# Sixteen more tokens served by gathered rows in a two-layer trunk, and chunks split two ahead

## The chip, the cores and the metric

The kernel runs on one core of one Trainium2 chip. The time is the device time of one execution in microseconds (us), from runs on the chip. The engines are PE (TensorE, matmuls; PEld is its weight load), DVE (VectorE), ACT (ScalarE), POOL (GpSimd) and SP (SyncE, which issues loads); a name with q behind it (ACTq, SPq) is an engine's issue of DMAs.

## What is computed

The reference is a two-layer trunk on 512 tokens of width 1024. Each layer adds a mixer (attention, a short convolution, gated linear attention) and then a PEER block, which takes most of the time:

```python
def peer(xn, w_q, keys1, keys2, u, v):
    q = (xt @ w_q).reshape(T, PEER_HEADS, 2, PEER_HALF)
    ...
    v1, i1 = lax.top_k(s1, PEER_TOPK)
    v2, i2 = lax.top_k(s2, PEER_TOPK)
    cand = (v1[..., :, None] + v2[..., None, :]).reshape(...)
    sc, ci = lax.top_k(cand, PEER_TOPK)
    ...
    experts = (e1 * PEER_NKEYS + e2).reshape(T, hk)
    gates = jax.nn.softmax(sc, axis=-1).reshape(T, hk)
    ...
        ub = jnp.take(u, eb, axis=0)
        hb = jax.nn.gelu(jnp.einsum('tkd,td->tk', ub, xb), approximate=False)
        vb = jnp.take(v, eb, axis=0)
        return jnp.einsum('tk,tkd->td', gb * hb, vb)
```

Every token picks 128 of 16384 experts (8 heads of 16). An expert has one row of u and one of v, 1024 wide. The inner value of an expert is gelu of the token's dot product with its u row; the output is the sum of the v rows, weighted with gate times inner value.

## The kernel before, in words

**Two ways through PEER.** For tokens 0 to 383 (three blocks of 128, TD = 384) the kernel is dense: it works out the inner values of all 16384 experts, in 128 chunks of 128 experts, and multiplies them with a gate matrix that is zero where an expert was not picked. For tokens 384 to 511 (block 3) it gathers the picked rows: `gathered` (L739) fetches 128 u rows, one for each of a token's picks, by an indirect DMA on POOL's queue (L735), takes the dot product with the normed token (`xg`) on DVE (L743), and then fetches 128 v rows and adds them up in `yacc` on DVE (L752). Four row buffers are in flight (NROW).

**Matmuls in three parts.** `mm3` (L73) makes one float32 product of three: high times high (L75), low or high parts crossed (L76, L77). The high part is ACT's copy of the raw tile, the low part DVE's subtraction (`split`, L649 to L651). So a chunk of hidden values (`hidden`, L659) is 8 x 3 = 24 matmuls, with the u chunk as weights and 384 tokens as columns, into one of two PSUM tiles of pool psB (`psh`), which ACT's Gelu then moves to a tile `ht` (L665).

**First loop** (L785 on, c from 0 to NPRE + LAG - 1 = 74). In each turn: load u chunk c+3 on SP's queue, split chunk c+1, `hidden(c)`, and for c under 72 store the result to DRAM (H, L789, on ACT's queue). Around that, DVE works through a generator `routing`: top-16 and routing of a token block (`route`), then for 16 tokens at a time a `gate_matrix`: four one-hot multiplies on DVE (L984 to L987), 32 matmuls into `psg` (L993, L994), four ACT copies to `stg` (L996) and a store into G in DRAM (L997, 512-byte pieces, 1 MB). Each yield of the generator says what it costs DVE, and a turn goes on until the sum passes `DVE_STEP * (c + 1)`. A step's matmuls and its store come out when the generator is resumed. Once block 3 is routed, `tick(RATE[0])` sends RATE[0] gathered rows a turn.

**Second loop** (L858 on, 128 turns). Turn i adds chunk order[i] to six PSUM tiles `pv`: 3 x 2 x 3 = 18 matmuls of 512 columns, weights `wh`, `wl` (gate times inner value, L833, L835) and columns `vh`, `vl` (the v chunk, L821, L826). The first 56 chunks in the order are 72 to 127, whose hidden values are computed three turns ahead in this loop; the others come back from H. G is read eight chunks at a time (`load_g`, L811), which has to wait for all stores into G. A turn also sends gathered rows: 2.8 in the first 56 turns, then 0.88. What is left is run after the loop, then block 3 gets `yacc` (L879), its sum of squares is taken on ACT (L173) and rsqrt on DVE (L161 to L168); the last two chunks are added block by block. The next layer's norm takes block 3 first (ORDER, L185, transposes L189 into `psn`); at the end of the kernel the scale into `fy` (L1006) and the store do.

**What sets the order.** Most instructions stand in program order on their engine: `pin` holds an instruction to the order in which it was written, `free` leaves it to the scheduler, and rows of a tick are put behind the last low part. Each engine runs its own list in order, so a wait holds all that is behind it. The buffers: three u highs and lows (NUW), three raw u (NUR), six `ht` (NHT), two `wh` and `wl` (NW).

## Time and profile before

| | us |
|---|---|
| median of 3 runs | 3046.72 (3039.78 to 3049.19) |
| the profiled execution | 3044.03 |
| its span, first to last instruction | 3042.3 |
| PE busy in it | 2971.3 |
| DVE busy in it | 2443.7 |
| ACT busy in it | 1268.9 |
| POOL busy in it | 736.2 |

The profile is of one execution: its span is the time from the first to the last instruction, 1.7 us less than the time of that execution, and 4.4 us less than the median of the runs. Matmuls are pipelined, so the busy time of one is longer than the distance to the next start; the distance tells the pace. A busy share is a mean over stages with different limits.

### The profile page before, as it was taken

The numbers are of one execution on the slowest core, as the hardware profiler recorded it, in microseconds if no ns is written. First come the engines' busy times: TensorE is split into PE (matmuls) and PEld (weight loads), VectorE is DVE, ScalarE is ACT, GpSimd is POOL, SyncE is SP. The second block draws the span as 40 slices with busy tenths as digits, with TensorE's granted clock in tenths as the row PEclk, the third lists the DMA queues.
The fourth block names the chain that finished last, engine by engine and source line by source line (L and its number), as shares of the span: only waits on it lengthen the run. The fifth ranks groups of instructions, "written<-read, shape, count | busy, mean of one in ns | idle before, by whom it ended". The sixth has DMA issues, their size and how long they took to land.

```text
span 3042.3 us, 45583 instructions
## 1 busy us (share of the span) xinstructions
PE 2971.3 (98%) x16742; PEld 2659.7 (87%) x16742; DVE 2443.7 (80%) x5057; ACT 1268.9 (42%) x1874; POOL 736.2 (24%) x553
## 2 busy tenths in 40 slices
PE   7999999999999999999999999999999999999998
PEld 7977889999999998788889788999999999988886
DVE  5766999987788787877766769999868788878777
ACT  5343346556333333333353533555553333323333
POOL 0000000222455544322100000002225555542221
PEclk9999999999999999999999999999999999999999
DMA  4212247799989888999722212578999899889996
GB/s 122 67 58 70 98 143 255 271 307 335 348 321 333 322 324 309 362 335 330 282 78 67 73 65 96 169 242 295 314 351 335 323 321 338 330 295 353 333 348 232
DMA packets 335696, 756.64 MB, mean 249 GB/s; under 512 B 31568, under 2 KB 192240, under 8 KB 331376
## 3 DMA queue, kind: packets, MB, share of 16 engines
q1 hardware_dynamic: 141936, 406.60, 37.2%
q0 software_dynamic: 73728, 268.47, 24.7%
q10 hardware_dynamic: 119808, 78.66, 8.2%
q8 instruction: 131, 2.15, 0.3%
q14 instruction: 93, 0.76, 0.1%
HBM read 672.89 MB, written 80.74 MB: 248 GB/s over the span
## 4 chain that ended last, share of the span: by engine, by line
PE 79%; DVE 6%; issue 4%; ACT 4%; DMA 3%; POOL 2%; ACTq 1%; SPq 0%; POOLq 0%; DVEq 0%
PE pv L77 10%; PE pv L76 10%; PE pv L75 10%; PE psh L75 9%; PE psh L77 9%; PE psh L76 9%; PE psp L77 2%; PE psp L76 2%; PE psp L75 2%; PE psq L76 2%; PE psq L77 2%; PE psq L75 2%; POOL row L735 2%; DMA row<-in_v_rows,idx 1%; ACTq L789 1%
## 5 line engine op out<-in xcount | busy, mean ns | idle before, releaser
L735 POOL DMA_INDIRECT row<-in_u_rows,idx x256 | 389.1, 1520 | 1326.3 <-DVE si L893 679.3
L75 PE MATMUL psh<-ahi,uh 128*128 128x384 f32 x2048 | 694.5, 339 | 10.1 <-ACT ht L665 10.1
L77 PE MATMUL psh<-ahi,ul 128*128 128x384 f32 x2048 | 689.2, 337 | 6.6 <-DVE ul L651 6.6
L76 PE MATMUL psh<-alo,uh 128*128 128x384 f32 x2048 | 688.4, 336 | 0.0
L75 PE MATMUL pv<-vh,wh 128*128 128x512 f32 x1536 | 597.7, 390 | 10.4 <-ACT wh L835 10.4
L77 PE MATMUL pv<-vh,wl 128*128 128x512 f32 x1536 | 600.4, 391 | 0.0
L76 PE MATMUL pv<-vl,wh 128*128 128x512 f32 x1536 | 599.9, 391 | 0.0
L735 POOL DMA_INDIRECT row<-in_v_rows,idx x256 | 329.1, 1286 | 604.1 <-DVE yacc L752 568.3
L650 ACT CAST uh<-uraw 128x1024 fp32r<-128x1024 f32 x288 | 302.7, 1053 | 319.8 <-PE psh L76 154.4
L651 DVE TENSOR_TENSOR ul<-uraw,uh 128x1024 fp32r<-128x1024 f32 x288 | 350.4, 1220 | 98.9 <-ACT uh L650 85.5
L75 PEld LDWEIGHTS psh<-ahi,uh 128*128 128x128 f32 x2048 | 387.1, 189 | 16.2 <-ACT ht L665 11.9
L77 PEld LDWEIGHTS psh<-ahi,ul 128*128 128x128 f32 x2048 | 386.6, 189 | 7.2 <-DVE ul L651 7.2
L76 PEld LDWEIGHTS psh<-alo,uh 128*128 128x128 f32 x2048 | 387.0, 189 | 4.1
L821 DVE TENSOR_TENSOR vl<-vraw,vh 128x1024 fp32r<-128x1024 f32 x256 | 312.5, 1221 | 86.5 <-issue 66.5
L665 ACT ACTIVATE ht<-psh 128x384 f32<-128x384 f32 x256 | 125.3, 489 | 613.6 <-PE psh L77 601.1
L75 PEld LDWEIGHTS pv<-vh,wh 128*128 128x128 f32 x1536 | 288.9, 188 | 69.3 <-ACT wh L835 12.0
L77 PEld LDWEIGHTS pv<-vh,wl 128*128 128x128 f32 x1536 | 288.9, 188 | 61.6 <-DVE wl L821 1.1
L76 PEld LDWEIGHTS pv<-vl,wh 128*128 128x128 f32 x1536 | 289.0, 188 | 58.6 <-DVE vl L821 0.5
L752 DVE SCALAR_TENSOR_TENSOR yacc<-row,wk,yacc 128x1024 f32<-128x1024 f32 x254 | 325.7, 1282 | 11.0 <-DMA row<-in_v_rows,idx 9.5
L743 DVE SCALAR_TENSOR_TENSOR gscr<-row,xg 128x1024 f32<-128x1024 f32 x256 | 312.5, 1221 | 13.0 <-DMA row<-in_u_rows,idx 11.3
L835 ACT CAST wh<-ht 128x384 fp32r<-128x384 f32 x256 | 130.7, 510 | 383.2 <-PE pv L76 236.3
L826 ACT CAST vh<-vraw 128x1024 fp32r<-128x1024 f32 x256 | 268.7, 1050 | 26.6 <-DMA vraw<-in_v_rows 24.5
(289 smaller groups left out, 4406.8 us busy)
## 6 DMA issues: line engine op xcount, KB each, us to landing
uraw<-in_peer_u SPq DMA_DIRECT2D x256, 512.0 KB
vraw<-in_v_rows SPq DMA_DIRECT2D x256, 512.0 KB
G<-stg ACTq DMA_DIRECT2D x48, 1024.0 KB
g<-G SPq DMA_DIRECT2D x32, 1536.0 KB
H<-ht ACTq DMA_DIRECT2D x144, 192.0 KB
ht<-H SPq DMA_DIRECT2D x144, 192.0 KB
wraw<-in_w_in SPq DMA_DIRECT2D x96, 256.0 KB
uraw<-in_peer_w_q SPq DMA_DIRECT2D x32, 512.0 KB
```

Of the source, the lines that this page charges most:

```text
L75: mm(ps, ah, bh, start=first, stop=False)
L76: mm(ps, ah, bl, start=False, stop=False)
L77: mm(ps, al, bh, start=False, stop=last)
L650: pin(nc.scalar.copy(hi, src))
L651: self.last = pin(nc.vector.tensor_tensor(lo, src, hi.bitcast(F32), op=OP.subtract))
L665: pin(nc.scalar.activation(hs[c], ps, AF.Gelu))
L735: nc.gpsimd.indirect_dma_start(out=r, out_offset=None, in_=ins[name], in_offset=bass.IndirectOffsetOnAxis(ap=idx[:, k:k + 1], axis=0))
L743: nc.vector.scalar_tensor_tensor(sc, r, 1.0, xg, op0=OP.mult, op1=OP.mult, accum_out=hd[:, k:k + 1])
L752: nc.vector.scalar_tensor_tensor(yacc, r, wk[:, k:k + 1], yacc, op0=OP.mult, op1=OP.add)
L821: self.last = pin(nc.vector.tensor_tensor(lo, src, hi.bitcast(F32), op=OP.subtract))
L826: pin(nc.scalar.copy(vh[c], vs[c]))
L835: pin(nc.scalar.copy(wh[c], hs[c]))
```

## The change

The first 16 tokens of block 0 (NX) leave the hidden matmuls, which go from 384 to 368 columns. Their 128 u rows a token are gathered instead, in 16 steps of 128 rows: `regroup` spreads 16 tokens by 128 picks over 128 partitions by small DMAs on POOL's queue, `xx` holds the normed tokens eight times over, and `extra` makes dot, Gelu and gate and brings the products back. The products then enter the gate matrix of these tokens in place of the gates, as three bfloat16 parts, and in the second loop the 16 columns of `ht` are copied from `g` by ACT instead of multiplied. Apart from that, u is loaded four and split two chunks ahead (one more buffer), `w_hi` is made two turns ahead (one more `wh`), G is read one turn sooner, the first loop takes 80 + 3 chunks instead of 72 + 3, and the rates are others.

```diff
-NPRE = 72
+NPRE = 80
-NHT = 6
+NHT = 5
-NUW = 3
+NUW = 4
-RATE = (0.8, 2.8, 0.88)
-DVE_STEP = 2.72
+RATE = (0.7, 2.8, 0.95)
+DVE_STEP = 2.62
+NX = 16
...
+            xx = pp.tile([P, D], F32, tag="yacc", name="xx")
...
             def hidden(c, pin=pin):
                 uh, ul = uw.pop(c)
-                ps = self.psB.tile([P, TD], F32, tag="b", name="psh")
+                ps = self.psB.tile([P, TD - NX], F32, tag="b", name="psh")
                 for k in range(KD):
-                    self.mm3(ps, uh[:, k], ul[:, k], xh[:, k, 0:TD], xl[:, k, 0:TD], k == 0, k == KD - 1)
+                    self.mm3(ps, uh[:, k], ul[:, k], xh[:, k, NX:TD], xl[:, k, NX:TD], k == 0, k == KD - 1)
                 hs[c] = spare.pop() if spare else new_h()
-                pin(nc.scalar.activation(hs[c], ps, AF.Gelu))
+                pin(nc.scalar.activation(hs[c][:, NX:], ps, AF.Gelu))
...
+                    nc.vector.scalar_tensor_tensor(xx[0:NX], self.x[0:NX, 0], self.rs[0][0:NX], xg[0:NX],
+                                                   op0=OP.mult, op1=OP.mult)
+                    n = NX
+                    while n < P:
+                        nc.gpsimd.dma_start(xx[n:2 * n], xx[0:n])
+                        n *= 2
...
+            def dot(k, xg=xg, hd=hd, idx=idx):
+                r = rows("u_rows", k, idx)
+                sc = gp.tile([P, D], F32, tag="gscr", name="gscr", bufs=1)
+                nc.vector.scalar_tensor_tensor(sc, r, 1.0, xg, op0=OP.mult, op1=OP.mult, accum_out=hd[:, k:k + 1])
...
+            def ahead(c):
+                load_u(c + 4)
+                split_u(c + 2, free)
+                hidden(c, free)
+                if c < NPRE:
+                    nc.scalar.dma_start(H[c], hs.pop(c)[:, NX:])
+
+            ahead(0)
+            best(NQ - 1)
...
+                def extra(gt):
...
+                    regroup(lambda p, s: nc.gpsimd.dma_start(ix[p], idx0[0:NX, s]))
+                    regroup(lambda p, s: nc.gpsimd.dma_start(gx[p], gt[0:NX, s]))
+                    yield 0.1
+                    for k in range(w):
+                        dot(k, xx, hx, ix)
+                        yield 1.25
+                    nc.scalar.activation(hx, hx, AF.Gelu)
+                    nc.vector.tensor_tensor(hx, hx, gx, op=OP.mult)
+                    regroup(lambda p, s: nc.gpsimd.dma_start(wx[0:NX, s], hx[p]))
+                    yield 0.3
...
                         for bt in range(P // TBAT):
-                            yield from self.gate_matrix(tb * (P // TBAT) + bt, E1, E2, GH, GL, G, hp)
+                            if tb == 0 and bt < NX // TBAT:
+                                continue
+                            yield from self.gate_matrix(tb * (P // TBAT) + bt, E1, E2, (GH, GL), G, hp)
+                            for _ in range(3):
+                                yield next(more, 0)
+                        if tb == 1:
+                            for w in more:
+                                yield w
+                            for bt in range(NX // TBAT):
+                                yield from self.gate_matrix(bt, E1, E2, [w3[:, i] for i in range(3)], G, hp, BF16, 1.0)
...
                 for c in range(NPRE + LAG):
-                    load_u(c + 3)
-                    split_u(c + 1, free)
-                    hidden(c, free)
-                    if c == 0:
-                        best(NQ - 1)
-                    if c < NPRE:
-                        nc.scalar.dma_start(H[c], hs.pop(c))
+                    if c:
+                        ahead(c)
...
-                pin(nc.vector.tensor_tensor(htv, htv, gt[c // GE][:, :, c % GE * TBAT:c % GE * TBAT + TBAT], op=OP.mult))
-                wh[c] = vp.tile([P, TD], F32R, tag="wh", name="wh", bufs=NW)
+                pin(nc.scalar.copy(htv[:, 0:b], gv[:, 0:b]))
+                pin(nc.vector.tensor_tensor(htv[:, b:], htv[:, b:], gv[:, b:], op=OP.mult))
+                wh[c] = vp.tile([P, TD], F32R, tag="wh", name="wh", bufs=NW + 1)
                 pin(nc.scalar.copy(wh[c], hs[c]))
...
-            for i in range(3):
-                at(load_v, i)
+            for i in range(4):
+                if i < 3:
+                    at(load_v, i)
                 at(load_g, i)
+            at(w_hi, 0)
             at(v_hi, 0)
+            at(w_hi, 1)
             at(v_hi, 1)
             at(v_lo, 0)
-            at(w_hi, 0)
             at(w_lo, 0)
             for i, c in enumerate(order):
                 rate = RATE[1] if c >= NPRE else RATE[2]
-                load_u(NPRE + i + LAG + 3)
+                load_u(NPRE + i + LAG + 4)
                 at(load_v, i + 3)
-                at(load_g, i + 3)
-                split_u(NPRE + i + LAG + 1)
+                at(load_g, i + 4)
+                split_u(NPRE + i + LAG + 2)
                 if i + LAG < NF:
                     hidden(order[i + LAG])
                 tick(rate / 2)
-                at(w_hi, i + 1)
-                at(v_hi, i + 2)
                 at(v_lo, i + 1)
                 at(w_lo, i + 1)
+                at(w_hi, i + 2)
+                at(v_hi, i + 2)
```

`gate_matrix` takes a list of parts, multiplies the one-hot tile by each and adds as many matmuls for a token; its yield is now 1.15 for each of its DVE steps (4.6 for two parts, as before). The pool of the query stage is closed before the routing pools open, and `yacc` takes the buffer of `xx`.

## Rows read from the trace of the kernel before

**Rows 1.** The page: span; busy us (share) xinstructions of each engine.
```profile
span 3042.3 us, 45583 instructions
...
PE 2971.3 (98%) x16742; PEld 2659.7 (87%) x16742; DVE 2443.7 (80%) x5057; ACT 1268.9 (42%) x1874; POOL 736.2 (24%) x553
```

**Rows 2.** Timeline of PE: start and duration (us), engine, line, operation, operands, shape.
```profile
159.35 0.28 PE L77 MATMUL psp<-wh,alo 128*128 128x256 f32 x1
...
160.42 0.28 PE L77 MATMUL psp<-wh,alo 128*128 128x256 f32 x1
...
599.32 0.33 PE L75 MATMUL psh<-ahi,uh 128*128 128x384 f32 x1
...
602.27 0.34 PE L77 MATMUL psh<-ahi,ul 128*128 128x384 f32 x1
...
1299.43 0.39 PE L75 MATMUL pv<-vh,wh 128*128 128x512 f32 x1
...
1302.83 0.39 PE L75 MATMUL pv<-vh,wh 128*128 128x512 f32 x1
```

**Rows 3.** Waits of PE: waiter <- releaser: us in total, times, longest.
```profile
PE pv L75 <- ACT wh L835: 10.4, 4, 4.6
PE psh L75 <- ACT ht L665: 10.1, 5, 3.3
PE psh L77 <- DVE ul L651: 6.6, 2, 3.3
```

**Rows 4.** Windows, instructions on psh: stretch, length, busy us (count), clock, DMA share, GB/s.
```profile
392.70:434.30 41.60, 36.07 (x192) 34.67 (x192) 3.40 (x7) 0.96 0.35 131
740.40:773.70 33.30, 30.92 (x168) 30.48 (x168) 3.28 (x7) 0.95 0.96 353
2249.30:2280.10 30.80, 29.58 (x168) 29.05 (x168) 2.93 (x6) 1.00 1.02 377
```

**Rows 5.** Groups by line: instructions xcount | busy us, mean ns | idle before, releaser.
```profile
L75 PE MATMUL psh<-ahi,uh 128*128 128x384 f32 x2048 | 694.5, 339 | 10.1 <-ACT ht L665 10.1
...
L752 DVE SCALAR_TENSOR_TENSOR yacc<-row,wk,yacc 128x1024 f32<-128x1024 f32 x254 | 325.7, 1282 | 11.0 <-DMA row<-in_v_rows,idx 9.5
...
L826 ACT CAST vh<-vraw 128x1024 fp32r<-128x1024 f32 x256 | 268.7, 1050 | 26.6 <-DMA vraw<-in_v_rows 24.5
```

**Rows 6.** Windows, all instructions: busy us (count) of PE, PEld, DVE, ACT, POOL.
```profile
392.70:434.30 41.60, 36.99 (x204) 35.85 (x203) 40.28 (x161) 17.05 (x24) 0.00 (x0) 0.96 0.35 131
```

**Rows 7.** Tiles psg, G, g near the first hand-over: count, ns min/median/max, first to last start.
```profile
L994 PE MATMUL psg<-ohl,ohb x80: 218/218/218, 701.8 to 740.4; 128*128 128x128 f16 x80
...
L997 ACTq DMA_DIRECT2D G<-stg x24: 377/377/423, 443.7 to 744.5; - x24
L811 SPq DMA_DIRECT2D g<-G x2: 330/356/383, 758.6 to 808.1; - x2
...
L833 DVE TENSOR_TENSOR ht<-ht,g x7: 552/553/554, 772.4 to 812.3; 128x384 f32<-128x384 f32 x7
```

**Rows 8.** The chain that ended last: start, us on the chain, what (two DMAs).
```profile
2252.72 12.94 DMA G<-stg
...
1211.04 7.68 DMA row<-in_v_rows,idx
```

**Rows 9.** Timeline around the end of both layers: start, us, engine, line, instruction.
```profile
1506.43 1.28 DVE L752 SCALAR_TENSOR_TENSOR yacc<-row,wk,yacc 128x1024 f32<-128x1024 f32 x1
...
1514.38 0.55 DVE L821 TENSOR_TENSOR wl<-ht,wh 128x384 fp32r<-128x384 f32 x1
...
1521.24 0.39 PE L77 MATMUL pv<-vh,wl 128*128 128x512 f32 x1
1521.47 1.03 PE L189 MATMUL psn<-ident,kT 128*128 128x128 f32 x8
...
3030.08 0.39 PE L77 MATMUL pv<-vh,wl 128*128 128x512 f32 x1
...
3037.23 1.28 DVE L1006 SCALAR_TENSOR_TENSOR fy<-x,ry,fg 128x1024 f32<-128x1024 f32 x1
```

More of the change, by code (lines that the diff above doesn't have):

```diff
@@ L95, in setup @@
         self.rstd = {}
[L96 removed]
+        self.rs = {tb: cp.tile([P, 1], F32, name=f"rs{tb}") for tb in (0, TB - 1)}
         self.ident = cp.tile([P, P], F32, name="ident")
@@ L181, in norm_T @@
             rstd = self.rstd.pop(tb) if tb in self.rstd else self.x_rstd(tb, sq)
-            if keep is not None and tb == TB - 1:
-                nc.vector.tensor_copy(keep, rstd)
+            if keep is not None and tb in keep:
+                nc.vector.tensor_copy(keep[tb], rstd)
             xn = xns[j % len(xns)]
@@ L729, in peer, with rows @@
             wk = pp.tile([P, P], F32, name="wk")
-            yacc = pp.tile([P, D], F32, name="yacc")
-            gp = pc.enter_context(tc.tile_pool(name="gather", bufs=1, reuse_waits="tile"))
-            def rows(name, k):
+            def rows(name, k, idx=idx):
                 r = gp.tile([P, D], F32, tag="row", name="row", bufs=NROW)
@@ L753, in gathered @@
                     yield
+            yacc = None
             side = gathered()
@@ L768, in routing @@
                 def routing():
+                    more = None
                     for tb in range(TB):
@@ new lines, in gate_matrix @@
+        t0 = bt * TBAT
+        ng = OHT // 2
+        tok = lambda t: bc(t[:, t0:t0 + OHT], [[2, ng], [0, P], [1, 2]])
+        io = bc(self.iota2, [[0, ng], [2, P], [1, 2]])
+        B = hp.tile([P, ng, P, 2], dt, tag="ohb", name="ohb")
+        A = hp.tile([P, ng, P, 2], F16, tag="oha", name="oha", bufs=1)
+        nc.vector.tensor_tensor(A, io, tok(E1), op=OP.is_equal)
+        nc.vector.tensor_tensor(B, io, tok(E2), op=OP.is_equal)
+        AW = []
+        for i, part in enumerate(parts):
+            AW.append(hp.tile([P, ng, P, 2], dt, tag=("ohh", "ohl")[i % 2], name="ohw"))
+            nc.vector.tensor_tensor(AW[i], A, tok(part), op=OP.mult)
@@ new lines, in gate_matrix @@
+        yield 1.15 * (2 + len(parts))
+        for g in range(OHT // 4):
+            ps = self.psA.tile([P, 4, P], F32, tag="a", name="psg")
+            for j in range(4):
+                at = (slice(None), g * 2 + j // 2, slice(None), j % 2)
+                for i, a in enumerate(AW):
+                    nc.tensor.matmul(ps[:, j], B[at], a[at], start=i == 0, stop=i == len(AW) - 1)
+            nc.scalar.activation(stg[:, :, g * 4:g * 4 + 4].rearrange("p e t -> p t e"), ps, AF.Copy, scale=scale)
```

84 lines of the change are left out of this document (46 added, 38 removed).

## The prediction

> **What bounds the kernel now.** I read the page first: TensorE is busy for 98% of the span [rows 1]. A busy PE is not yet a PE at its peak, so I then took the distance between the starts of neighbouring matmuls from the timeline of PE [rows 2]. The reader is to see three constant cadences: ten matmuls of 256 columns start in nine steps from 159.35 to 160.42 us (0.119 us each), eighteen of 384 columns in seventeen steps from 599.32 to 602.27 us (0.1735 us), sixteen of 512 columns in fifteen steps from 1299.43 to 1302.83 us (0.2267 us). Each column costs 0.42 ns in both intervals. So the time follows what PE streams, wherever PE is fed. Where it isn't, the view of waits names the causes: evictions by ACT (ht), lows by DVE (ul), and wh [rows 3]. These sums are small, but a window shows more than a sum of waits. From 392.7 to 434.3 us PE did 192 matmuls into psh, eight chunks, which at 0.1735 us are 33.3 us of the 41.6; the granted clock there was 0.96, so part of the loss is a stretch at the lower level, 1.2 GHz, behind the idle time [rows 4].
>
> **The change part by part.** The profiled execution took 3044.0 us with a span of 3042.3; the median of the three runs is 3046.7. The sum is made against 3044.0.
>
> *Columns.* Each layer has 128 chunks of 24 matmuls into psh, 6144 in both (2048 for each of three lines [rows 5]); each loses 16 columns, 16 x 0.42 = 6.7 ns: **-41 us**. If something other than columns set the cadence, it is 0 (a rival below).
>
> The Trainium skill, page "TensorE: Matmul & The Clock Gate", section "Back-to-back issue gap", gives for sustained streams about 81 ns at 128 columns and 131 ns at 512. By an estimate from it, 16 columns are worth (131-81)/24 = 2.1 ns, the term -13 us and the total 28 us more. The trace disagrees: 227 ns at 512 columns [rows 2].
>
> *Extra gate matmuls.* The sixteen tokens' matrix has three parts, so 16 more matmuls of 128 columns in each layer. The cadences of rows 2 go on to about 0.066 us at 128 columns: 2 x 16 x 0.066 = **+2 us**. VectorE gets 16 dots of about 1.3 us a layer (a yacc step of the same shape takes 1.28 [rows 5]), 21 us, and one more multiply; the first loop is eight chunks longer, 32 us of PE, and with a step of 2.62 plus a split of about 1.2 asks 3.8 us of DVE in a chunk of at least 4.0 us before row work goes live. I cost them at nothing; without that cover they are up to 42 us. The small DMAs of the regrouping and of xx stand on POOL's queue before it has rows to fetch, the H stores are shorter but eight more a layer, the extra copies of 16 columns run on ACT, which was busy for 17.05 of 41.6 us at the entry [rows 6]: nothing.
>
> *Entry of the first loop.* DVE does the last top-16 and a route there while the lows wait, 8.3 us lost a layer [rows 4]. Splitting two ahead gives one chunk of slack more. But DVE is busy there for 40.28 of 41.6 us [rows 6]: its work, not its order alone, is late, so I take half: **-8 us** in both layers (bounds -16 and 0).
>
> *ACT's queue.* The waits on ht come where ACT is held between a G store, an H store and the route's Exp. Deeper splits help PE past a late uh, but not past a full psB. Of the 10.1 us [rows 3] I take **-3** (bounds -10 and 0).
>
> *Hand-over to the second loop.* In the kernel before, the generator's last gate matrix is emitted at c = 68 of 75, so seven hidden chunks, 29.1 us, lie between its last matmul and the first pv; the stretches measured 33.3 and 30.8 us, 5.9 us lost in both layers [rows 4]. Counting the yields with the new step 2.62, the last matrix comes out at c = 79 of 83, so only chunks 80 to 83 cover: 4 x 24 x 0.1668 = 16.0 us. What must fit: from the last psg matmul to the issue of the G store 4.1 and 3.4 us (740.4 to 744.5; 2249.3 to 2252.7), the store 14.1 and 12.9 us until the load of g may go, the load itself, then multiply, wh and vh [rows 4, 7, 8]. The load is 1.57 MB; at the 377 GB/s of that stretch 4.2 us [rows 4], at most 13.8 (758.6 to 772.4 [rows 7]); I take 6.5, near the first, since DVE did not wait for it there. From the first multiply to pv it was 1.3 us (772.4 to the end of the stretch at 773.7), and the vh cast of 1.05 [rows 5] now stands behind it. Chain: 3.8 + 13.5 + 6.5 + 2.3 = 26 us against 16, so 10 us idle and near 2 us of lower clock after it, 24 in two layers, less 5.9: **+18** (bounds +4, if the next hidden chunks move ahead of pv; +30, if the load is slow). Behind the waiting load on SP's queue stand vraw, uraw; behind the waiting multiply on DVE the splits.
>
> Loads of u, g and H go out one turn sooner on SP, with the same two turns to their use: nothing.
>
> *End of the hidden chunks.* PE waits 4.6 us a layer for wh, with rows still coming at 2.8 a chunk. wh is now made two ahead. The row rate is unchanged there, so **-4** in both (bounds -9 and +3).
>
> *Leftover rows.* Counting the ticks: before, 38 + 56 x 2.8 + 0.88 a chunk reach 256 at i = 124, and the last yacc indeed ran at 1506.43 us [rows 9]. After: 33 + 48 x 2.8 + 80 x 0.95 = 243.3, so 244 done at the end, and of the 256 some 14 come after the last wl. That wl ended at 1514.9, 6.4 us before the last pv at 1521.24 [rows 9]. At DVE's own pace (1.2 to 1.3 us) they end 11 us after the last pv. At the gather's pace, four in flight and 7.68 us for one in a full stretch [rows 8] plus the 1.28 of the step that frees its buffer, 2.2 us a row, the ten that are not yet there end near +23. The second loop's loads are over by then, so the queues are emptier than in that row: I take +14, nearer to DVE's pace. Then add, square and scale, three passes over 128x1024 at 1.05 to 1.28 us each [rows 5], with nine small steps of rsqrt between them (an estimate of 0.2 us each): block 3 is ready 19.5 us after the last pv. The 0.07 rows a turn more in the second loop are 0.09 us of DVE in a turn of 4.08: nothing. The next layer takes block 3 first, and psn started at 1521.47, at once. Its own waits and one block that may go ahead absorb 5.5: **+14** (8 to 22). At the end of the kernel: the last fy started 3037.23 and the last pv 3030.08, so the span ended 3.7 us after that fy and 12 after the last pv [rows 1, 9]; now 19.5 + 3.7 = 23: **+11** (6 to 20).
>
> Sum: -41 + 2 - 8 - 3 + 18 - 4 + 14 + 11 = **-11 us**: 3033 us, 0.45% below the median.
>
> **The rivals.** *PE stays fed* (chance 0.25): hidden chunk 84 goes ahead of the late pv, gathers in the quiet tail keep DVE's pace, and a block other than 3 starts the layer. Hand-over +6, tails +10: -41 + 2 - 10 - 5 + 6 - 6 + 10 = -44, 3000 us. For it: PE's program need not keep my order. Against: dots and gelu around it are held in program order. *Rows at gather's pace* (0.20), the slower side: each leftover row takes 2.2 us, so the two tails are +26 and +20 instead of 25 together, -11 + 21 = +10, 3054 us. It decides from a row pace of about 2 us. For it: gathers took 7.68 us [rows 8]. Against: the queues are empty there. *Weights set the pace* (0.03): no gain from columns, 3033 + 41 = 3074 us. Against it are the 256-column matmuls, with the same weight loads at 0.119 us [rows 2]. By the sentence above on the Trainium skill's page "TensorE: Matmul & The Clock Gate" it would be 3061. *Two ahead does nothing* (0.10): the entry stays bound by DVE's top-16, ACT's queue as before: 3033 + 11 = 3044 us.
>
> **How the numbers follow.** The forecast has 0.42, with 3015 to 3050 for itself. A measurement of this kernel tells about 0.3%, 9 us, from no change. Faster by more: half of the forecast and the whole first rival, 0.46. Within: the rest of the forecast, half of the slow tail, the last rival, 0.31. Slower: 0.23. The range runs from 3003 (the first rival) to 3060 (above the slow tail).
>
> **What would show it.** The cadence of psh falls to 0.167 us. Eight chunks at the entry take under 38 us. Between the last psg and the first pv PE idles some 10 us with g's load waiting for G. Twelve or more yacc steps stand behind the last wl, and psn of the second layer starts 10 to 20 us after the last pv. It is wrong if the first pv follows the hidden chunks at once, if the tail is short, or if the second loop, at 0.95 rows a chunk, no longer keeps 0.2267 us a matmul.

## The result, and the profile after

The changed kernel takes 3068.20 us (median of six runs, 3059.6 to 3072.35) against 3047.39 for the kernel before in the same sessions: a ratio of 1.0073, 95% interval 1.006 to 1.0086. It is 0.7% slower. The forecast was 3033 us, its range ended at 3060. The profiled execution took 3072.35 us, the highest of the six, with a span of 3070.5, so 28.2 us more than the span of before; between the medians it is 20.8 us.

Engine rows of the page after, against [rows 1]. PE is busy for 34 us less than before, in a span that is 28 us longer: the columns did go, and other time came.

```profile
span 3070.5 us, 46432 instructions
...
PE 2936.9 (96%) x16776; PEld 2620.6 (85%) x16776; DVE 2477.6 (81%) x5143; ACT 1298.8 (42%) x2134; POOL 743.3 (24%) x639
```

The timeline of PE, 36 matmuls of 368 columns apart, against [rows 2]: 6.00 / 36 = 0.1667 us each instead of 0.1735. Over 6144 matmuls that is 42 us, as forecast.

```profile
598.79 0.33 PE L77 MATMUL psh<-alo,uh 128*128 128x368 f32 x1
...
604.79 0.33 PE L77 MATMUL psh<-alo,uh 128*128 128x368 f32 x1
```

Windows of the changed kernel (stretch, length, busy us and count by engine, clock, DMA share, GB/s), the same stages as in [rows 4], instructions on psh: the first eight hidden chunks, then last psg to first pv in both layers. The entry is down from 41.6 to 35.2 us and keeps the full clock.

```profile
392.40:427.60 35.20, 32.56 (x193) 31.83 (x193) 3.30 (x7) 1.00 0.43 138
...
783.60:806.60 23.00, 18.08 (x107) 17.80 (x107) 1.45 (x3) 0.95 0.93 322
2310.60:2332.10 21.50, 18.08 (x107) 17.80 (x107) 1.92 (x4) 1.00 0.98 351
```

The stretch between, from the ninth chunk to the last psg, all instructions (PE, PEld, DVE, ACT, POOL). First the kernel before, then the changed one. Length less PE's busy time is PE's idle time: 3.5 and 2.7 us before, 13.7 and 12.3 after. This is new, and the prediction has it at nothing.

```profile
434.30:740.40 306.10, 302.62 (x2239) 298.33 (x2239) 279.03 (x494) 184.80 (x231) 53.16 (x37) 0.99 0.85 283
1943.80:2249.30 305.50, 302.79 (x2239) 298.44 (x2239) 279.71 (x496) 185.44 (x232) 53.52 (x37) 0.99 0.86 284
```

```profile
427.60:783.60 356.00, 342.35 (x2522) 336.19 (x2521) 316.92 (x560) 200.34 (x258) 88.07 (x68) 0.99 0.87 288
1956.80:2310.60 353.80, 341.50 (x2522) 335.47 (x2521) 316.13 (x559) 199.20 (x256) 86.40 (x68) 0.99 0.86 288
```

Waits of PE in the changed kernel, against [rows 3]. The wait on wh is gone. The wait on ht has grown, those on psg and rtr in the first loop have all but come new, and one towers over all: psn, the next layer's first transposes, 24.1 us (the other 12.9 are the start of the kernel).

```profile
PE psn L190 <- DVE kT L186: 37.0, 2, 24.1
PE psh L76 <- ACT ht L667: 13.0, 8, 3.3
...
PE psg L1067 <- ACT stg L1068: 5.9, 9, 2.3
...
PE psg L1067 <- DVE ohw L1060: 4.0, 4, 1.5
...
PE rtr L1038 <- DVE ex L1014: 3.0, 2, 1.7
```

Where that wait comes from stands in the chain that ended last, at the end of the first layer (start, us on the chain, what). The last pv started at 1511.22. The rows left over are on the chain one behind the other: two gathers of 5.1 us, one of 5.8, the last step into yacc at 1528.33, then x, and only then the load of the next layer's first weights (wraw). The first psv of layer two started at 1537.54, 26.3 us after the last pv. Before, psn followed the last pv at once, at 1521.47 [rows 9], and psv came at 1522.75, 1.5 us after that pv. The timelines first (changed kernel, then the first psv of before), then the chain.

```profile
1511.22 0.39 PE L78 MATMUL pv<-vh,wl 128*128 128x512 f32 x1
...
1537.54 0.58 PE L76 MATMUL psv<-wh,ahi 128*128 128x256 f32 x1
```

```profile
1522.75 0.38 PE L75 MATMUL psv<-wh,ahi 128*128 128x256 f32 x1 [0.24 <-ACT ahi L191]
```

```profile
1508.17 5.15 DMA row<-in_v_rows,idx
...
1513.55 5.11 DMA row<-in_v_rows,idx
...
1522.42 5.82 DMA row<-in_v_rows,idx
...
1528.33 1.29 DVE yacc L766
1529.65 1.22 DVE x L952
1530.91 0.37 SPq L243
...
1531.32 3.07 DMA wraw<-in_w_in
```

At the end of the kernel (timeline: start, us, engine, line; in brackets the idle time before and its releaser) the last pv started at 3036.42. Ten steps into yacc come after it, ACT stands for 27 us before the first square, and the four scales into fy follow. Last pv to the end of the span: 34.1 us, against 12.2 before.

```profile
3036.42 0.39 PE L78 MATMUL pv<-vh,wl 128*128 128x512 f32 x1
...
3052.72 1.28 DVE L766 SCALAR_TENSOR_TENSOR yacc<-row,wk,yacc 128x1024 f32<-128x1024 f32 x1 [0.33 <-DMA row<-in_v_rows,idx]
...
3055.30 1.06 ACT L174 ACTIVATE gscr<-x 128x1024 f32<-128x1024 f32 x1 [27.19 <-DVE x L952]
...
3065.45 1.28 DVE L1078 SCALAR_TENSOR_TENSOR fy<-x,ry,fg 128x1024 f32<-128x1024 f32 x1 [0.46 <-DMA out<-fy]
```

So two things were to be explained: 24.8 + 21.9 = 46.7 us behind the two loops, and some 20 us of new idle time in the first loops.

### The profile page after: what moved, and what is told of

Read it like the earlier page. It is cut to its first block, busy times and chain, and to the rows that moved or that the text cites. A ratio compares the mean times of both kernels' runs of the same rounds, so it can differ in the third digit from the quotient of the medians.

```text
span 3070.5 us, 46432 instructions
## 1 busy us (share of the span) xinstructions
PE 2936.9 (96%) x16776; PEld 2620.6 (85%) x16776; DVE 2477.6 (81%) x5143; ACT 1298.8 (42%) x2134; POOL 743.3 (24%) x639
## 4 chain that ended last, share of the span: by engine, by line
PE 43%; issue 25%; DVE 11%; DMA 9%; POOL 7%; ACT 3%; ACTq 1%; SPq 0%; POOLq 0%; DVEq 0%
POOL row L744 7%; PE pv L76 4%; PE pv L78 4%; PE pv L77 4%; PE psh L76 4%; PE psh L78 4%; PE psh L77 4%; DMA row<-in_v_rows,idx 3%; DMA row<-in_u_rows,idx 3%; PE psp L78 2%; PE psp L77 2%; PE psp L76 2%; PE psq L76 2%; PE psq L77 2%; PE psq L78 2%
## 5 line engine op out<-in xcount | busy, mean ns | idle before, releaser
L76 PE MATMUL psh<-ahi,uh 128*128 128x368 f32 x2048 | 682.1, 333 | 13.0 <-ACT ht L667 13.0
L78 PE MATMUL psh<-ahi,ul 128*128 128x368 f32 x2048 | 675.9, 330 | 3.6 <-DVE ul L653 3.6
L77 PE MATMUL psh<-alo,uh 128*128 128x368 f32 x2048 | 675.6, 330 | 0.0
L744 POOL DMA_INDIRECT row<-in_u_rows,idx x256 | 360.4, 1408 | 761.9 <-DVE gscr L751 673.0
L744 POOL DMA_INDIRECT row<-in_v_rows,idx x256 | 283.1, 1106 | 626.6 <-DVE yacc L766 584.3
L667 ACT ACTIVATE ht<-psh 128x368 f32<-128x368 f32 x256 | 121.3, 474 | 258.7 <-PE psh L78 245.6
```

The source lines that it names most:

```text
L76: mm(ps, ah, bh, start=first, stop=False)
L77: mm(ps, ah, bl, start=False, stop=False)
L78: mm(ps, al, bh, start=False, stop=last)
L667: pin(nc.scalar.activation(hs[c][:, NX:], ps, AF.Gelu))
L744: nc.gpsimd.indirect_dma_start(out=r, out_offset=None, in_=ins[name], in_offset=bass.IndirectOffsetOnAxis(ap=idx[:, k:k + 1], axis=0))
```

## The experiments

All ratios are to the kernel before, run beside it on the same chip.

| run | edit | median us | ratio, 95% |
|---|---|---|---|
| changed kernel | | 3068.2 | 1.0073 (1.006 to 1.0086) |
| e1 | rows in time | 3022.1 | 0.9929 (0.9909 to 0.9949) |
| e2 | kernel before, rows late | 3090.8 | 1.0149 (1.0132 to 1.0166) |
| e3 | block 3 last | 3059.8 | 1.0047 (1.003 to 1.0064) |
| e4 | dots later | 3061.1 | 1.0054 (1.0036 to 1.0072) |
| e5 | e1, one chunk ahead | 3043.5 | 0.9996 (0.9987 to 1.0006) |
| e6 | e1, no gathers for the sixteen tokens | 3009.6 | 0.9885 (0.9868 to 0.9901) |
| e7 | e6, no dots either | 3002.0 | 0.9849 (0.9832 to 0.9867) |
| e8 | three row buffers | 3178.9 | 1.0444 (1.0426 to 1.0461) |
| e9 | e1, dots later | 3023.0 | 0.9921 (0.9905 to 0.9938) |
| e10 | e1, dots spread | 3036.6 | 0.9966 (0.9953 to 0.998) |
| e11 | e1, step 2.75 | 3019.0 | 0.9921 (0.9898 to 0.9945) |
| e12 | e9, wtr later | 3022.0 | 0.9922 (0.9903 to 0.9941) |
| e13, e15 | e12, added products on DVE | 3025.8, 3025.3 | 0.9933 (0.9912 to 0.9955), 0.9928 (0.9911 to 0.9944) |
| e14 | e12, step 2.75 | 3025.6 | 0.9929 (0.9914 to 0.9944) |
| e16 | e12, lows in another form | 3022.3 | 0.9925 (0.991 to 0.9939) |
| e17 | e1, lows in another form | 3019.0 | 0.9912 (0.9897 to 0.9928) |

**Rows in time, and rows late alone.** The first run takes the late rows out of the changed kernel, the second puts them into the kernel before.

```diff
-RATE = (0.7, 2.8, 0.95)
+RATE = (0.7, 2.8, 1.15)
```

> The changed kernel with 1.15 instead of 0.95 rows a turn after the first 48 turns of the second loop, so that the 256th row falls due near turn 125 and none is left behind the loop. Theory (late rows): what the change lost against its forecast lies behind the loops, 23 us between the layers and 22 us at the end; this takes them back, 3068 - 45 = about 3023 us, last pv to first psv about 3 us, last pv to the end of the span about 12 us. Rival (VectorE is full): the rows do not fit beside the second loop's multiplies and lows at 1.15 a turn, a turn takes longer than 4.08 us, and what the tails give back is lost in the loop: 3055 to 3068 us, with waits of PE on wl or vl.

```diff
 (the kernel before)
-RATE = (0.8, 2.8, 0.88)
+RATE = (0.8, 2.8, 0.68)
```

> The kernel before with 0.68 instead of 0.88 rows a turn after the first 56 turns of the second loop: 38 + 56 x 2.8 + 72 x 0.68 = 243.8, so about twelve rows are left behind the loop, as in the changed kernel, and nothing else of the change is in it. Theory (late rows): the two tails alone cost the 45 us, so 3047 + 45 = about 3092 us. Rival (the tail is only as long as the rows, 14 and 11 us as forecast): 3072 us. Second rival (the tail is long in the changed kernel because of something else of the change, wh or the queues): under 3062 us.

Both came out at the theory's number: 3022 and 3091 us. In e1 (timeline of PE) psn starts 0.2 us after the last pv and psv 1.5 us after it; at the end of the kernel the last fy starts 7.2 us after the last pv. VectorE had room for nearly all the rows: the part of the second loop behind the hidden chunks took 351 and 348 us, against 346.5 and 346.7 in the changed kernel, so 5.8 us of the 46.7 were paid there.

```profile
1508.77 0.39 PE L78 MATMUL pv<-vh,wl 128*128 128x512 f32 x1
1509.01 1.03 PE L190 MATMUL psn<-ident,kT 128*128 128x128 f32 x8
1510.28 0.38 PE L76 MATMUL psv<-wh,ahi 128*128 128x256 f32 x1 [0.24 <-ACT ahi L192]
```

In e2, with nothing of the change in it but late rows, PE idles 23 us before psn again, and the two tails are 25.2 and 32.2 us.

```profile
1524.39 0.39 PE L77 MATMUL pv<-vh,wl 128*128 128x512 f32 x1
1547.79 1.97 PE L189 MATMUL psn<-ident,kT 128*128 128x128 f32 x8 [23.02 <-DVE kT L185]
```

**What makes the tail long.** One idea was ScalarE's order: all squares stand behind block 3's. The other was the pace of the gathers.

```diff
-ORDER = (3, 0, 1, 2)
+ORDER = (0, 1, 2, 3)
...
-            for _ in side:
-                pass
-            nc.vector.tensor_tensor(self.x[:, 3], self.x[:, 3], yacc, op=OP.add)
-            self.rstd[3] = self.x_rstd(3, sq)
             for tb in range(TD // P):
...
                 self.rstd[tb] = self.x_rstd(tb, sq)
+            for _ in side:
+                pass
+            nc.vector.tensor_tensor(self.x[:, 3], self.x[:, 3], yacc, op=OP.add)
+            self.rstd[3] = self.x_rstd(3, sq)
```

> The changed kernel, rows late as they are, but the leftover rows, the addition to block 3 and its square are written behind the three dense blocks, and the next layer and the final scale take block 3 last. Theory (ScalarE's order): most of what the tail costs beyond the rows themselves comes from the squares of blocks 0 to 2, which stand behind block 3's square in ScalarE's list, so all four blocks wait for the rows; with this, three blocks go on at once, the first psv starts under 8 us after the last pv, and the time is 15 to 25 us under the changed kernel's 3068. Rival (the rows alone): block 3 is as late as before and everything waits for it further on, 3060 to 3068 us.

The theory of ScalarE's order fell as far as the time goes. The squares of blocks 0 to 2 were done by 1509, their norms began at 1513, and still psv came 28.0 us after the last pv (at 1506.42), and the end 35.1 us after the last one. The norm's small steps now stand between the rows on DVE and hold the buffers longer, and PE waits at psv for the weights. At the end the order does count: with one scale instead of four behind block 3, the span ends 9.9 us after the last row instead of 16.5; but that row came 25.2 us after the last pv instead of 17.6. These could be loaded only when x had taken yacc, in this run as in the chain above (1529.65 + 1.21, then SP at 1530.89). The median is 8 us under the changed kernel's; that isn't in the tails but in the first loops, whose code is the same in both (first psh to first pv: 414.2 and 410.5 us in the changed kernel, 409.5 and 405.8 in e3). What makes them differ is open.

```profile
1529.65 1.21 DVE L960 TENSOR_TENSOR x<-x,yacc 128x1024 f32<-128x1024 f32 x1
...
1534.47 0.80 PE L76 MATMUL psv<-wh,ahi 128*128 128x256 f32 x2 [5.78 <-ACT wh L81]
```

```diff
-NROW = 4
+NROW = 3
```

> The changed kernel with its late rows, three row buffers instead of four. In it a leftover row was fetched every 1.79 us, and 5.1 (the gather) + 1.28 (the step that frees the buffer) + 0.94 (its issue) = 7.3 us go round four buffers. Theory (gather's pace): with three buffers a row takes 7.3 / 3 = 2.4 us; the ten or so rows of each tail cost 6 us more, and the time is 3068 + 12 = about 3080 us. Rival (VectorE's order, with the additions between the rows, sets the pace): within 4 us of 3068.

The tails are 31.9 and 40.0 us, 5.5 and 6.0 more than in the changed kernel, as the theory of the gather's pace has it: a step into yacc every 2.28 us (seven intervals, 3139.15 to 3155.14) where four buffers gave 1.70 (seven, 3040.79 to 3052.72). Three times 2.28 and four times 1.70 are both 6.8 us. That is one round of a buffer: 5.1 us from issue to landing, 1.28 of the step, 0.4 between. The expectation had 7.3, since it counted the issue of 0.94 twice: the 5.1 begin with it. The other 99 us were not expected by either. In the second loop rows come too late for 2.8 a turn when only three are in flight: DVE waits 156 us for rows of block 3 in the whole run (58 in the changed kernel), the lows behind it come late (waits of PE, below), and the hidden part of the second loop takes 388 instead of 358 us in each layer, the part behind it 359 and 361 instead of 347.

```profile
PE pv L77 <- DVE vl L889: 57.5, 30, 6.5
```

**Two chunks ahead.** On top of e1:

```diff
-NUW = 4
+NUW = 3
...
-                load_u(c + 4)
-                split_u(c + 2, free)
+                load_u(c + 3)
+                split_u(c + 1, free)
```

> The kernel of the run with 1.15 rows a turn (3022 us), with u loaded three and split one chunk ahead again, three u highs and lows; all else of the change stays. Theory (two ahead is worth the entry): the first eight hidden chunks took 35 us instead of 41.6 because the lows were ready before VectorE's last top-16; with one ahead they take 38 to 41 us again in both layers, about 3030 us. Rival (the gain came from writing the first chunk ahead of the last top-16): 35 to 36 us and 3019 to 3025 us. Second rival (a cast of u that is written two chunks early holds ScalarE while the raw chunk is still on its way, and with it the Gelu behind): faster, 3005 to 3015 us, with less wait of PE on ht in the first loop.

The first eight chunks took 41.8 and 41.0 us again, so the entry's gain is the second chunk of slack, not the earlier first chunk. The clock of that stretch is below full again, 0.92, as in [rows 4]. In time it cost 21 us. 12.5 of it are the two entries (e1 35.1 each); the rest is lateness later in the first loop (first psh to first pv: 418.8 and 422.7 us, e1 407.3 and 408.8). So without the second chunk ahead, e1 would be no faster than the kernel before. The second rival, that casting early does harm, is out.

```profile
391.50:433.40 41.90, 35.81 (x193) 34.64 (x192) 3.31 (x7) 0.92 0.37 125
```

**The new idle time in the first loop.** On top of e1:

```diff
-                        dot(k, xx, hx, ix)
+                        sc = gp.tile([P, D], F32, tag="gscr", name="gscr", bufs=1)
+                        nc.vector.scalar_tensor_tensor(sc, xg, 1.0, xx, op0=OP.mult, op1=OP.mult, accum_out=hx[:, k:k + 1])
```

> The kernel of the run with 1.15 rows a turn (3022 us), where the dots of the sixteen tokens read a tile that is already there instead of gathered u rows: sixteen indirect loads a layer are left out (so the inner values of these tokens are others), VectorE's work stays. Some 10 us a layer of PE's waits in the first loop are new against the kernel before. Theory (the gathers: their lateness on VectorE or their traffic beside the loads of u): 10 to 20 us faster, 3002 to 3012 us, and few waits of ScalarE on uraw. Rival (VectorE's extra work or other parts of the change): within 5 us of 3022.

```diff
-                        dot(k, xx, hx, ix)
+                        if k == 0:
+                            nc.vector.memset(hx, 0.0)
```

> As the run without gathers, but the sixteen dots themselves are left out too (their sums are set to zero), the generator's pace as it was: 16 x 1.28 = 20.5 us less of VectorE's work a layer. Theory (the gathers cost, not the work): the same as the run without gathers, within 4 us. Rival (VectorE's work is what delays the one-hots and lows): another 8 to 20 us faster than the run without gathers. Second rival (neither: the small copies, the three-part gate matrix and ScalarE's share): both within 5 us of 3022.

Without the gathers the kernel is 12.5 us faster, with VectorE's work unchanged. The windows (ninth chunk to last psg; first e1, then e6) show it in the same stretch: PE idles 9.8 and 11.8 us in e1, 3.8 and 7.3 in e6, which takes back 10.5 of the 15.4 us that e1 idles more than the kernel before. Without the dots as well the median is 7.6 us lower still, but the two intervals touch. Its profile doesn't settle it (PE idles 4.9 and 6.7 us), as it is of that run's slowest execution, 3008 us. Whether VectorE's work costs something of its own is left open; by the medians the gathers are the larger part.

```profile
428.00:778.00 350.00, 340.17 (x2525) 334.02 (x2522) 316.20 (x559) 199.34 (x257) 88.02 (x68) 1.00 0.87 292
...
1924.50:2277.00 352.50, 340.68 (x2524) 333.82 (x2522) 316.28 (x559) 199.71 (x257) 87.43 (x68) 1.00 0.86 289
```

```profile
428.90:772.80 343.90, 340.11 (x2534) 335.54 (x2532) 316.12 (x560) 200.63 (x258) 62.07 (x52) 1.00 0.82 272
1917.60:2263.90 346.30, 339.05 (x2523) 333.75 (x2522) 316.03 (x560) 199.00 (x257) 59.35 (x52) 1.00 0.83 271
```

How do gathers cost PE time? The first idea was that dots wait. In the changed kernel DVE stands before the first dot, with one-hots and lows behind it: the first gather is issued at 439.08, its issue alone takes 4.42 us, and DVE's last instruction before the dot started at 441.39.

```profile
439.08 4.42 POOL L744 DMA_INDIRECT row<-in_u_rows,ix  x1 [2.78 <-DMA ix<-idx]
```

```profile
441.39 1.22 DVE L1060 TENSOR_TENSOR ohw<-oha,GL 128x2048 f16<-128x2048 f16 x1
449.75 1.23 DVE L751 SCALAR_TENSOR_TENSOR gscr<-row,xx 128x1024 f32<-128x1024 f32 x1 [7.14 <-DMA row<-in_u_rows,ix]
```

The plain mend is to start the dots later (e4 on the changed kernel, e9 on e1), or to ask for rows more slowly (e10, on e1).

```diff
                         if tb == 0:
                             more = extra(gt)
+                            yield next(more, 0)
...
-                            for _ in range(3):
+                            for _ in range(0 if tb == 0 and bt < 3 else 3):
                                 yield next(more, 0)
```

> The changed kernel, rows late as they are, but of the generator of the sixteen tokens only the small copies are issued at once; its dots begin two gate matrices later (about 15 us of VectorE's work), so that the first gathered rows have landed. Theory (VectorE waits for rows): some 20 us over the two layers were lost in the first loop because dots that wait for gathered rows hold the one-hot multiplies and the lows behind them; this takes back 10 to 20 us, 3048 to 3058 us, and the waits of DVE on row in the first loop (9.2 us in three) go. Rival (the work, not the wait): the dots cost the same wherever they stand, 3064 to 3070 us.

> Both mends together: 1.15 rows a turn in the last 80 turns and the sixteen tokens' dots begun two gate matrices after their small copies. Theory (two separate losses: tails, 45 us, and waits of VectorE for gathered rows in the first loop, some 7 us by the run that moved the dots alone): 3022 - 7 = about 3015 us. Rival (what the moved dots gave back came from the tails or from the spread of the runs): 3020 to 3026 us.

In e10 the last range is `range(0 if tb == 0 and bt < 2 else 2)`.

> 1.15 rows a turn, the small copies at once, the dots one gate matrix later and two instead of three to a matrix, so that a row is asked for every 4.2 instead of 2.8 us of VectorE's time while G is being stored. Leaving the gathers out altogether gave 12.5 us (3022 to 3010). Theory (rows that come too fast for the gather): most of that, 3010 to 3016 us. Rival (their traffic beside the loads of u and the stores of G, wherever they stand): 3018 to 3026 us.

The mend failed. e4 is 7 us under the changed kernel, but in the traces its tails alone are 6.6 us shorter (22.4 and 31.4 instead of 26.3 and 34.1), e9 is where e1 was, and e10 is 14 us worse. The timelines of e9 say why the wait stayed: with nothing but one-hots and lows on DVE, the issue of the first gather takes 10.29 us instead of 4.42. It ends 0.9 us after DVE's list has run dry (447.17 + 1.22), and DVE waits 7.29 us for the row all the same.

```profile
438.98 10.29 POOL L744 DMA_INDIRECT row<-in_u_rows,ix  x1 [2.58 <-DMA ix<-idx]
```

```profile
447.17 1.22 DVE L1061 TENSOR_TENSOR ohw<-oha,GL 128x2048 f16<-128x2048 f16 x1
455.68 1.23 DVE L751 SCALAR_TENSOR_TENSOR gscr<-row,xx 128x1024 f32<-128x1024 f32 x1 [7.29 <-DMA row<-in_u_rows,ix]
```

Layer one of e4 went otherwise (in its layer two a dot waited 7.1 us again). There too DVE had nothing but one-hots and lows, one behind the other from 438.44 to 449.79, yet the first four gathers were issued in 1.93 to 1.97 us each, and no dot waited for its row. PE idled 10.4 us from the ninth chunk to the last psg all the same, where e1 has 9.8: the first sign that this wait is not what costs the time.

```profile
439.74 1.93 POOL L744 DMA_INDIRECT row<-in_u_rows,ix  x1 [2.04 <-DMA ix<-idx]
```

```profile
449.79 1.22 DVE L751 SCALAR_TENSOR_TENSOR gscr<-row,xx 128x1024 f32<-128x1024 f32 x1
```

```profile
428.60:781.20 352.60, 342.17 (x2523) 336.58 (x2522) 318.50 (x562) 201.11 (x258) 86.02 (x69) 0.99 0.87 293
```

In e10 a second wait joins it: PE comes to the transpose of the products (wtr) before the small copies to wx are through, which stand on POOL's queue behind block 3's gathers, 9.5 us once (in an execution 18 us above the median of that run). e9 has 5.2 us of it. So e12 moves wtr as well, and e13 and e15 let VectorE do something else between the one-hots.

```diff
                     regroup(lambda p, s: nc.gpsimd.dma_start(wx[0:NX, s], hx[p]))
                     yield 0.3
+                    for _ in range(6):
+                        yield 0
```

> As the run with both mends (3023 us: 1.15 rows a turn, dots two gate matrices later), and the transpose that brings the sixteen tokens' products back (tile wtr) two gate matrices later still, since in that run PE stood 5.2 us in two waits before it for the small copies to wx. Theory (moving the dots gave nothing because it moved a wait from VectorE to PE's wtr): that wait goes, 3022 - 5 = about 3017 us. Rival (the wait of VectorE for the first row is still there, 7.3 us a layer, and is what counts): 3020 to 3026 us.

```diff
+                def apart():
+                    sc = gp.tile([P, D], F32, tag="gscr", name="gscr", bufs=1)
+                    nc.vector.scalar_tensor_tensor(sc, xg, 1.0, xg, op0=OP.mult, op1=OP.mult, accum_out=hd[:, 0:1])
...
-            nc.vector.tensor_tensor(AW[i], A, tok(part), op=OP.mult)
+            one = nc.vector.tensor_tensor(AW[i], A, tok(part), op=OP.mult)
+            if free is not None:
+                with self.tc.issue_after(one.ins):
+                    free()
```

> As the run before it, with four more products of xg with itself on VectorE (1.2 us each, results unused) set between the one-hot multiplies of the first two gate matrices. What is to be told apart: the first gather of the sixteen tokens was issued over 4.4 us in the changed kernel and over 10.3 us where its dots were moved, and in both ended 0.9 us after VectorE's gapless list of one-hots and lows had run dry. Theory (two-operand tensor_tensor instructions of VectorE keep POOL from writing the gather's descriptors, a scalar_tensor_tensor does not): the first gather's issue takes under 3 us, the 7.3 us wait of VectorE for the row goes in both layers, and the time is about the run before it, 2 to 8 us less (14 us of waits less 10 us of added work, of which some is hidden). Rival (the first gather is long for a reason of its own, the first of its kind or the copies ahead of it): issue still 4 to 10 us and the wait still there; the time 0 to 10 us more.

> As the run before last but with the four added products held to their places, one behind each second-stage one-hot multiply of the third and fourth matrix, the stretch in which the first gather waited for 10 us (the last time they had been placed in the query stage, so VectorE's list there was as gapless as before, and that run told nothing of them). Theory (tensor_tensor keeps POOL from writing the gather's descriptors, scalar_tensor_tensor lets it): the first gather's issue falls from 10.2 to under 4 us, and VectorE's wait of 7 us for the first row shrinks to under 2. Rival (a long first gather has another cause): the issue still takes about 10 us plus the added products, and the wait stays at 7. Time: 3022 us, less up to 8 by the theory, plus up to 10 by the rival.

In e12 the wait at wtr is gone and the time is the same, 3022 us: its rival. e13 has no `issue_after`; its products were placed at 347 us, in the query stage, and it told nothing. In e15 they stand in the right place (third and fourth matrix), and the issue is shorter, if not under 4 us: 4.56 us in layer one and 4.95 in layer two, the next three within 2 us each. No wait of DVE for the sixteen tokens' rows is left in the whole run.

```profile
438.69 4.56 POOL L744 DMA_INDIRECT row<-in_u_rows,ix  x1 [2.63 <-DMA ix<-idx]
...
595.52 26.13 POOL L744 DMA_INDIRECT row<-in_u_rows,idx  x1 [0.31 <-issue]
```

```profile
1936.80:2288.70 351.90, 341.44 (x2523) 336.54 (x2522) 321.61 (x569) 200.56 (x258) 90.37 (x69) 0.98 0.87 293
```

The time did not follow: 3025 us. In layer one PE now stood 11.1 us at wtr behind a gather of block 3, whose issue took 26.13 us. Layer two has neither that wait nor one for a row, and PE idled 10.5 us there (window), where e1 has 11.8. The added products are 5 us of DVE in it, so the run alone would not tell; with layer one of e4, which has no added work, it says that the dots' wait for rows is not the main cost. Which way the gathers cost their 12.5 us is open; their traffic beside the loads of u and the stores of G, the rival of e10, is held apart by no run. Two more runs tried the same without added work: the lows of u as scalar_tensor_tensor.

```diff
-                self.last = pin(nc.vector.tensor_tensor(lo, src, hi.bitcast(F32), op=OP.subtract))
+                self.last = pin(nc.vector.scalar_tensor_tensor(lo, src, 1.0, hi.bitcast(F32), op0=OP.mult, op1=OP.subtract))
```

> A version to beat both kernels, without added work: 1.15 rows a turn, dots and wtr later as in the run at 3022 us, and the lows of u written as scalar_tensor_tensor (raw times 1, minus high) instead of tensor_tensor, the same work and size. Theory (the added products of the last run let POOL in because they are scalar_tensor_tensor, and a low of the same kind does it for nothing): the first gather ends within 2.5 us of the start of a low, not 10, VectorE's wait for the first row falls from 7.4 to about 2 us, and the time to 3008 to 3016 us. Rival (what opened the way was the reading of an accumulator behind each product, or the low takes longer in this form): the issue takes 10 us again, or the lows take over 1.3 us, and 3020 to 3030 us.

> The kernel with 1.15 rows a turn (3022 us) and only the lows of u written as scalar_tensor_tensor; dots at once as in the changed kernel. Theory: gathers of all kinds find a way at every low; but the first dot follows the copies to ix too soon, VectorE's wait of 7 us for the first row stays at 5 to 7, later rows come up to 0.7 us sooner: 3014 to 3022 us. Rival (no difference): 3020 to 3026 us with issues as before.

In e16 a low in the new form started at the very moment of the issue, at 438.12, and another at 443.80, and the issue took 10.06 us as in e9: its rival. So it is not the form of the instruction. What the products of e15 have and the lows have not is the accumulator read behind each; but that this opens the way is not shown, and two rows above speak against it: in e4 gathers got through without one, and in e15 the issue of 26.13 us lasted past three dots with such a read. e17 is within the spread of e1.

```profile
438.12 10.06 POOL L744 DMA_INDIRECT row<-in_u_rows,ix  x1 [2.81 <-DMA ix<-idx]
```

**The hand-over.** The last two runs give the store and load of G more cover.

```diff
-DVE_STEP = 2.62
+DVE_STEP = 2.75
```

> 1.15 rows a turn and a step of 2.75 instead of 2.62 us of VectorE's work a turn in the first loop, so the last gate matrix comes out about four turns earlier and six or seven instead of three hidden chunks lie between its last matmul and the first pv. Theory (hand-over is bound by the store and load of G): the 7.9 and 5.5 us lost there fall to 2 to 3, and the time to 3014 to 3018 us. Rival (VectorE has no room for more in a turn, the lows come late instead): 3022 to 3035 us, with waits of PE on ul.

> A version to beat both kernels: 1.15 rows a turn, dots and wtr later, a step of 2.75 (which brought the loss at the hand-over from 6.3 and 3.7 to 1.0 and 0.4 us, while the time fell only from 3022 to 3019). Theory (losses that add up): 3010 to 3016 us. Rival (what the earlier gate matrices give at the hand-over they take in the first loop): 3018 to 3024 us.

In e11 PE no longer idles at the hand-over (28.43 us busy of 28.9, last psg to first pv), but the stretch before it, shorter by five microseconds, idles for 13.4 us instead of 9.8: what was gained at one place was lost at the other, and 3019 us is not told apart from e1. e14 is no better.

```profile
428.50:773.00 344.50, 331.15 (x2449) 324.21 (x2449) 310.54 (x554) 195.65 (x250) 85.95 (x67) 0.99 0.86 289
773.00:801.90 28.90, 28.43 (x174) 28.13 (x171) 13.39 (x17) 13.98 (x21) 3.75 (x4) 1.00 1.02 371
```

The version that beats both kernels is e1, one number of the change set otherwise: 0.7% under the kernel before. e9, e11, e12, e16 and e17 can't be told from it.

## Why the prediction was wrong

The forecast of -11 us against a measured +28 between the spans is off by 39 (by the medians, +21, off by 32). Two steps were far too cheap: the rows left over by 22 us, and the first loop behind its entry by some 31. A third, the hand-over, was 15 us too dear and hides part of that.

*Leftover rows: mis-sized.* The mechanism was right, and so was the count (ten rows not yet there at the last pv). The terms were +14 and +11; measured are +24.8 and +21.9, both beyond their bounds of 22 and 20. Three parts were short. I took the end of the rows at +14 us, nearer to DVE's own pace; the ten came at 1.81 and 1.72 us a row and ended at +18.4 and +17.6. Where DVE waited for rows the pace is the gather's, 6.8 us round four buffers, and e8 confirms it. Then I let the other waits and one block absorb 5.5 us of it at the layer's start; nothing was absorbed: ACT's order held the other blocks behind block 3, and in e3, where it did not, the next layer's weights were still loaded only when yacc had been read. And at the end of the kernel I added one scale and the store behind block 3; in truth four squares and four scales stand there, as ACT's order has it, 6.6 us more (16.5 against 9.9 in e3). The rival *Rows at gather's pace* had +26 and +20: it named the mechanism and nearly the size, and it had a chance of 0.20. Its row price was 2.2 us, taken from the loaded queue; the quiet tail gave 1.70, and what it overpriced in the rows it lacked behind them: that its 46 met the 46.7 is luck.

*Extra gate matmuls, DVE's part: "I cost them at nothing".* I gave the price if the cover was gone, up to 42 us, and then kept neither a case nor a chance for it. The two stretches between entry and last psg are 49.9 and 48.3 us longer, where 264 more matmuls into psh (44 us), less the columns that 1464 others lost (10), make 34 each: 30 us are new, against -1 forecast (+2 here and -3 for ACT's queue). 19.8 of them are idle time of PE: 7.2 more on ht, 5.7 on stg, 4.0 on the one-hots, 3.0 on rtr. Leaving out the gathers alone gave back 12.5 us, the dots another 7.6 that is not clear of noise. So the step that failed is "nothing": I asked whether the busy time of DVE fits, and gave the transfers that feed it no price. How they cost it stays open; a dot that waits for its row ahead of one-hots and lows was the idea, and e4 and e15 speak against it as the main way.

*Columns*: -41 forecast, -42 measured. By an estimate from the 131 and 81 ns that the Trainium skill's page "TensorE: Matmul & The Clock Gate" gives in "Back-to-back issue gap", 16 columns would be 2.1 ns. The trace disagrees: 0.1735 to 0.1667 us is 6.8 ns.

*Entry*: -8 forecast, and about -10 measured: 41.6 to 35.2 and 41.3 to 35.2 us, of which 1.3 each are columns. e5 shows that the second chunk ahead does it, and that it is worth 21 us in all with what it saves later. *Two ahead does nothing* is out.

*ACT's queue*: -3 forecast; the wait on ht rose from 10.1 to 13.0 us instead, all of it behind the entry.

*Hand-over*: +18 forecast. The cadence of psh gives 107 x 0.1667 = 17.8 us of the 23.0 and 21.5, so 8.9 us are lost in both layers, 3 more than the 5.9 before, not 18. PE did idle before g as foreseen. But the chain was shorter: the last store landed 5.0 us after its issue, not 13.5, though the load of g took 9.4 and not 6.5 (chain of waits, below). The cover was longer, 17.8 us and not 16, and the clock fell in one layer only.

```profile
789.76 5.03 DMA G<-stg
...
795.05 9.40 DMA g<-G
```

*End of the hidden chunks*: -4 forecast; 4.6 us a layer on wh have become 2.2 and 2.3 on vl, so about -5.

*The second loop* keeps its pace at 0.95 rows a turn, and nearly so at 1.15. *PE stays fed* and *Weights set the pace* did not happen. The sentence on the chances doesn't add up as it is worded: with half of the slow tail within 9 us, "within" is 0.41 and "slower" 0.13; the 0.31 and 0.23 count the whole slow tail as slower.

## What to carry to other kernels

Work that trickles along beside a loop must end inside it: a row that costs nothing beside the matmuls costs 1.7 us and more behind them, and everything that shares its memory or stands behind it in a list waits too. Count the due times of the last item when loop lengths or rates change. And when work is added to an engine that has room for it, busy time that fits is no reason to cost it at nothing: the gathers that feed it have a price too, 12.5 us here.

## What had not been expected of the hardware

**A gather's issue can be held beside VectorE, and not by a rule that these runs show.** An indirect DMA on POOL's queue was issued in 0.94 us beside an idle DVE, and also beside the yacc steps and additions of the tails. Beside dots, one-hots and lows it mostly took 1.68 us (eight in a row from 451.26 in the changed kernel). A few took far longer: the first gather of layer one 4.42 us in the changed kernel, 10.29 in e9, 10.06 in e16, and each of these ended 0.9 us after DVE's list had run dry; one in e15 took 26.13. The Trainium skill's page "SBUF — State Buffer", section "SBUF: two separate sides", says that POOL writes the descriptors of its DMAs itself, and that a VectorE instruction that holds the ports the two share keeps it from doing so for the length of that instruction. The issues of 1.68 us agree with that, the long ones do not: in e9 eight VectorE instructions ended, each with the next behind it, while one issue was held. What holds these few is open: in layer one of e4 a list of the same kind let the first four through in under 2 us each.

**Three rows in flight were too few.** One row buffer less cost 110 us over the changed kernel, far more than its 12 us in the tails.
